# Threshold attention in one kernel: the last group's queries picked out of resident tiles by one-hot products, one index instruction per group, and a new order of steps

## The chip, the cores and the metric

The kernel runs on one core of a Trainium2 chip. The metric is the device time of one execution in microseconds (us). Five engines matter: TensorE (PE) multiplies matrices, VectorE (DVE) and ScalarE (ACT) work on tiles, GpSimd (POOL) does small vector work and issues indirect DMAs (row gathers and scatters by a list of indices), and SyncE (SP) issues plain DMAs. PEld is TensorE's loading of weights.

## The reference

```python
def reference(Q, K, V, threshold):            # 8 x 12 x 512 x 64, threshold 0.1
    scale = 1.0 / np.sqrt(Q.shape[-1])
    scores = np.einsum('bhqd,bhkd->bhqk', Q, K) * scale
    weights = np.exp(scores - np.max(scores, axis=-1, keepdims=True))
    weights = weights / (np.sum(weights, axis=-1, keepdims=True) + 1e-10)
    weights = np.where(weights > threshold, weights, 0)
    weights = weights / (np.sum(weights, axis=-1, keepdims=True) + 1e-10)
    return np.einsum('bhqk,bhkd->bhqd', weights, V)
```

With random inputs few of the 512 weights of a query exceed 0.1. Most output rows are zero.

## The kernel before

The kernel uses that sparsity. The 96 heads are 48 pairs (`hp`, two heads); two pairs share one load (`q`, 24 of them), and four pairs form a group (`x`, 12 groups, 0 to 11). The work has three layers.

**For each load**: `k` and `q` bring K and Q in (SP's queue, L324 and L328); `qcast` (L314 on POOL, L312 on DVE) makes Q 16-bit; `ktr` and `qtr` (PE, L344 and L353) transpose; `kev` and `qev` (ACT L310 or DVE L312) copy the transposes out of PSUM, `kh` makes a 16-bit K; `bits` (DVE, L383) and `norms` (PE, L435) bound the vectors' norms; `z` (SP, L546) writes zeros over the output. K stays in float32, transposed, in the tiles `kt`.

**For each pair**: for each of four key tiles `t`, `sc` (PE, L393) makes scores in one of three double PSUM banks (`two`) and `ex` takes their exponential into a 16-bit tile `e`, on ACT (L402) or as an integer trick on DVE (L404). `g` (PE, L413: 32 products) sums the pair's four `e` tiles against a small weight matrix in one of two single PSUM banks (`one`), so that the sign of a maximum (`mx`, DVE, L419) says which queries may have a weight over the threshold.

**For each group**, the candidates, up to 32 for each pair, are treated exactly: `flags` (L425), `rank` (PE, L441 and L443) and `key` (L447) number them, `oh` (L452) makes one-hot columns, `idx` (PE, L463) multiplies these by row numbers. `idxev` (L467) and `base` (L472) write the indices. Then POOL's `gather` (L475) fetches the 128 query rows from memory, `split` (L481) puts each in its head's half, `xtr` (PE, L486) transposes, `xev` copies the result to `xq`, `xqk` (PE, L496, float32, four products side by side) scores them against `kt`, `xexp` (ACT, L501), `xcut` (L506) and `xkeep` (L510) find the kept key, `xvi` (L516) and `xoi` (L521) make the index of the V row and of the output row, and POOL's `gv` (L525) and `scatter` (L534) move that row of V to the output.

Group 11 comes last, and its steps stand one after the other at the kernel's end; only its `flags`, `rank`, `key` and `oh` are in two parts (pairs 0 to 2, pair 3).

At the end four `check` steps on DVE (L652, L653, L657, L658, L661) test that no pair had more than 32 candidates and no query more than one kept key; L669 (PE), L671 and L673 reduce the answer to one number, which every engine loads (L674) to branch to a slow loop or past it. The last barriers follow (L746).

Every step's place and, where it has a choice, its engine come from `ORDER`, a coded list of 1,080 entries that is read from first to last:

```python
        for i, choice in table:
            name, engs, deps, fn, takes, gives, mode = self.ops[i]
            for pool, key in takes:
                if (pool, key) not in self.held:
                    self.held[pool, key] = idle[pool].pop(0)
            pin(lambda: fn(engs[choice]))
```

`pin` fixes the order on each engine, so that an instruction that waits holds back all behind it on its engine. `fill` steps (PE, L550, two products of 512 columns on a tile of zeros) are also placed by the list. Decoded, the end of the old list is, engine by engine (`ex.47.2` is key tile 2 of pair 47):

```
PE   ... idx.9 g.42 sc.41.3 sc.43.1 sc.41.2 qtr.23 sc.45.2 sc.45.1 g.43 g.41 sc.45.3 sc.46.3 sc.45.0
     norms.10 xtr.9 rank.10 sc.47.3 sc.44.1 sc.46.1 g.45 sc.44.3 xqk.9 sc.47.0 sc.46.0 sc.46.2 idx.10
     g.44 sc.47.2 sc.47.1 g.46 g.47 rank.11.0 norms.11 rank.11.1 fill idx.11 fill xtr.10 fill xqk.10
     fill xtr.11 fill xqk.11 and 7 fill steps
ACT  ... ex.43.3 ex.43.2 ex.43.1 qev.23 ex.45.1 ex.45.3 ex.46.3 xev.9 ex.47.3 ex.44.1 ex.44.3 xexp.9
     ex.46.0 ex.46.2 ex.47.1 xev.10 xexp.10 xev.11 xexp.11
DVE  ... idxev.9 base.9 mx.42 ex.41.3 ex.41.2 ex.45.2 mx.43 mx.41 flags.10 ex.45.0 xkeep.8 key.10
     ex.46.1 xvi.8 mx.45 oh.10 xoi.8 ex.47.0 idxev.10 base.10 mx.44 ex.47.2 mx.46 flags.11.0 bits.23
     mx.47 key.11.0 flags.11.1 oh.11.0 key.11.1 oh.11.1 split.10 idxev.11 xcut.9 base.11 xkeep.9 xvi.9
     split.11 xcut.10 xkeep.10 xvi.10 xoi.10 xoi.9 check.1 xcut.11 xkeep.11 xvi.11 check.2 xoi.11
     check.0 check.3
POOL ... gather.9 scatter.6 kh.47 split.9 gv.8 gather.10 scatter.8 gather.11 gv.9 gv.10 scatter.9
     gv.11 scatter.10 scatter.11
```

## Time and profile before

| what | us |
|---|---|
| three runs | 198.43, 194.99, 198.74 |
| their median | 198.43 |
| the profiled execution's own time | 197.65 |
| its span, first to last instruction | 195.9 |

Of the span PE is busy 91%, DVE 84%, ACT 81% and POOL 53%. A busy PE is not PE at its peak, since the ends of its pipelined matmuls are modelled. A row of the timeline gives start, duration, engine, line, operation, tiles written and read, and a count where several were merged; in brackets stand the idle time before it and what ended that. Such a releaser is inferred, and of several the last by time is named.

### The profile page before, as it was taken

To read this page: it belongs to the slowest core of one execution; us is meant where nothing else is said; L and a number is where in the kernel's file an instruction comes from. 1 tells how busy PE (TensorE), PEld (TensorE's weight loads), DVE (VectorE), ACT (ScalarE), POOL (GpSimd) and SP (SyncE) were. 2 spreads that over 40 slices of the span, in tenths; PEclk is the share of its full clock that TensorE was granted. 3 is DMA by queue.
4 is the path that set the end of the run, shared out by engine and by line. 5 is a ranking of instruction groups with operands and counts; after the bars stand their busy time and mean duration, and the time that the engine had idled before them with its cause. 6 is when DMAs were issued, how large, how long until landed. Compare 5 with 4: busy or idle time off the path is not lost.

```text
span 195.9 us, 7813 instructions
## 1 busy us (share of the span) xinstructions
PE 177.8 (91%) x3256; PEld 112.0 (57%) x3270; DVE 165.1 (84%) x322; ACT 158.7 (81%) x191; POOL 103.4 (53%) x172
## 2 busy tenths in 40 slices
PE   7999989899989989999899999999899999999730
PEld 2447557656665646666566664766377656574200
DVE  5388999789887978998899999999899999985550
ACT  2799989689989888899799989999899998961200
POOL 5386566451284740475694645759662566243560
PEclk9999999999999999999999999999999999999995
DMA  5999999998959999979879999910690000000000
GB/s 169 274 311 250 278 264 275 309 273 198 272 194 319 360 291 358 301 210 296 240 225 310 375 295 322 282 48 5 177 359 16 12 1 10 3 11 0 9 6 9
DMA packets 68023, 38.77 MB, mean 198 GB/s; under 512 B 52356, under 2 KB 64720, under 8 KB 67984
## 3 DMA queue, kind: packets, MB, share of 16 engines
q1 hardware_dynamic: 66288, 37.23, 65.3%
q0 software_dynamic: 1152, 0.47, 1.0%
q8 instruction: 27, 0.44, 1.0%
q10 hardware_dynamic: 544, 0.52, 0.8%
q14 instruction: 12, 0.10, 0.1%
HBM read 25.95 MB, written 12.98 MB: 199 GB/s over the span
## 4 chain that ended last, share of the span: by engine, by line
PE 41%; DMA 21%; DVE 14%; POOL 7%; issue 6%; ACT 6%; SPq 1%; POOLq 0%; DVEq 0%; ACTq 0%
PE two L393 13%; PE one L413 11%; DMA q<-in_Q_dram 8%; DMA k<-in_K_dram 7%; DVE e L404 5%; DMA qs<-in_Q_dram,idx 5%; ACT e L402 4%; PE one L435 4%; POOL qh L314 3%; PE two L344 3%; PE one L496 3%; PE one L353 2%; PE one L463 2%; POOL qk L314 2%; PE one L550 2%
## 5 line engine op out<-in xcount | busy, mean ns | idle before, releaser
L402 ACT ACTIVATE e<-two 128x1024 bf16<-128x1024 f32 x131 | 126.7, 1032 | 10.0 <-PE two L393 7.9
L404 DVE TENSOR_SCALAR e<-two 128x1024 int16<-128x1024 f32 x61 | 74.2, 1218 | 10.0 <-PE two L393 7.6
L393 PE MATMUL two<-qk 64*128 64x512 f16 x384 | 61.4, 381 | 1.8 <-DVE e L404 0.2
L413 PEld LDWEIGHTS <-e 128*128 128x128 bf16 x1536 | 42.2, 96 | 10.6 <-issue 10.1
L413 PE MATMUL one<-gw,e 128*128 128x48 bf16 x1536 | 46.4, 183 | 0.5 <-DVE qk L312 0.3
L314 POOL CAST qh<-q 128x512 f16<-128x512 f32 x43 | 28.1, 670 | 15.0 <-DMA q<-in_Q_dram 9.4
L314 POOL CAST qk<-kt 128x512 f16<-128x512 f32 x42 | 27.1, 657 | 9.1 <-ACT kt L310 5.3
L393 PEld LDWEIGHTS <-qk 64*128 64x128 f16 x384 | 17.2, 94 | 23.5 <-issue 14.9
L475 POOL DMA_INDIRECT qs<-in_Q_dram,idx x12 | 14.2, 1186 | 27.2 <-DVE idx L467 10.4
L419 DVE TENSOR_REDUCE st<-one 128x8 f32<-128x320 f32 x48 | 22.9, 481 | 1.4 <-PE one L413 1.3
L550 PE MATMUL one<-spare 128*128 128x512 bf16 x66 | 20.2, 406 | 1.9 <-DVE spare L187 1.3
L310 ACT COPY kt<-two 128x1024 f32<-128x1024 f32 (+1 forms) x22 | 21.4, 979 | 0.6 <-PE two L344 0.5
L525 POOL DMA_INDIRECT vr<-in_V_dram,idx x12 | 12.6, 1049 | 12.8 <-DVE idx L516 8.4
L344 PEld LDWEIGHTS two<-identity_f,k 64*128 64x128 f32 x384 | 14.7, 138 | 7.6 <-ACT e L402 3.8
L344 PE MATMUL two<-identity_f,k 64*128 64x64 f32 x384 | 17.3, 227 | 1.7 <-DMA k<-in_K_dram 1.1
L383 DVE TENSOR_SCALAR v<-qk 128x1024 int32<-128x1024 int32 x24 | 17.5, 729 | 0.0
L312 DVE COPY qk<-one 128x1024 f16<-128x1024 f16 (+1 forms) x21 | 14.1, 670 | 3.5 <-PE one L353 3.3
L534 POOL DMA_INDIRECT out_dram<-vr,idx x12 | 12.9, 1075 | 7.6 <-DVE idx L521 4.5
L353 PE MATMUL one<-identity_h,qh 128*128 128x128 f16 x192 | 14.9, 220 | 0.4 <-POOL qh L314 0.3
L353 PEld LDWEIGHTS <-qh 128*128 128x128 f16 x192 | 11.2, 97 | 5.3 <-issue 3.3
L550 PEld LDWEIGHTS <-spare 128*128 128x128 bf16 x80 | 6.4, 102 | 11.7 <-issue 7.9
L435 PEld LDWEIGHTS <-v 128*128 128x128 bf16 x384 | 10.9, 96 | 3.7 <-issue 3.4
(79 smaller groups left out, 142.7 us busy)
## 6 DMA issues: line engine op xcount, KB each, us to landing
k<-in_K_dram SPq DMA_DIRECT2D x96, 128.0 KB, 4.5
out_dram<-zero SPq DMA_DIRECT2D x24, 512.0 KB, 5.8
q<-in_Q_dram SPq DMA_DIRECT2D x23, 512.0 KB, 5.6
q<-in_Q_dram ACTq DMA_DIRECT2D x2, 256.0 KB
qs<-in_Q_dram,idx POOLq DMA_INDIRECT x12, 4.7
vr<-in_V_dram,idx POOLq DMA_INDIRECT x12, 3.2
out_dram<-vr,idx POOLq DMA_INDIRECT x12, 2.8
```

The costliest lines, as they stand in the source:

```text
L310: nc.scalar.copy(dst, src)
L314: nc.gpsimd.tensor_copy(dst, src)
L344: nc.tensor.matmul(dst[:, i, c:c + D], lhsT=src[ps, n0 + n, r, :], rhs=identity_f32[ps, ps], is_transpose=True, start=True, stop=True)
L353: nc.tensor.matmul(dst[:, c:c + P], lhsT=src[:, n0 + n, r, :], rhs=identity_h[:], is_transpose=True, start=True, stop=True)
L383: nc.vector.tensor_scalar(v_b[at("v", q)][:].rearrange("p a n c -> p (a n c)").bitcast(i32), qk_b[at("qk", q)][:].rearrange("p a n c -> p ...
L393: nc.tensor.matmul(dst[:, h, :], lhsT=qk[ps, 1, n, t * P:(t + 1) * P], rhs=qk[ps, 0, n, :], start=True, stop=True)
L402: nc.scalar.activation(dst, src, ACTF.Exp, scale=scale)
L404: nc.vector.tensor_scalar(dst.bitcast(i16), src, scale * LOG2E * 128.0, 127.0 * 128.0, op0=ALU.mult, op1=ALU.add)
L413: nc.tensor.matmul(dst[:, c * GW:(c + 1) * GW], lhsT=e_b[at("e", (hp, t))][:, h, qt * P:(qt + 1) * P], rhs=gw[:, kind[hp, t], t, :], start ...
L419: nc.vector.tensor_reduce(st_b[at("st", x)][:, n, :], one[at("one", ("g", hp))][:, 0:C2 * GW].rearrange("p (c g) -> p c g", g=GW)[:, :, 0: ...
L435: nc.tensor.matmul(dst[:, c:c + 2], lhsT=v[:, w, n, r * P:(r + 1) * P], rhs=heads[:], start=True, stop=True)
L550: nc.tensor.matmul(one[at("one", ("fill", i))][:], lhsT=spare[:, 0:P], rhs=spare[:], start=True, stop=True)
```

## The change

**The last group's queries come from tiles that are in SBUF already.** For group 11 `idxev`, `gather`, `split` and `xtr` are gone. `oh` becomes four steps, one for each pair, into a float32 tile; `pick` (PE) multiplies the loaded Q tile by these columns, which gives the transposed query rows at once, 8 float32 products for each pair; `xev` and `xqk` are in two parts (pairs 0 to 2, pair 3). `idx` for the group is 32 float32 products of 6 columns instead of 8 16-bit ones of 4, and stands behind `xqk`, since only `gv` and `scatter` need its result. `flags`, `rank` and `key` are in four parts, and the norms' part of `key` is a step of its own, `size`. The Q tiles of loads 22 and 23 are held until their `pick`.

**`g` by key tile.** For pairs 44 to 47 `g` is four steps of 8 products, one for each `e` tile as it comes.

**One index instruction.** `xvi` and `xoi` become `xo`, which writes both columns; `base` has 6 columns.

**More buffers**: indices 3 to 8, V rows 3 to 6. A few constants are laid out anew (on POOL, at the start).

**A new `ORDER`** of 1,091 entries. Of the steps with a choice of engine these change: `kev` ACT/DVE 22/3 to 23/2, `qev` 4/21 to 2/23, `kh` POOL/DVE 42/4 to 44/2, `split` POOL/DVE 9/3 to 10/1, `xev` ACT/DVE 7/5 to 7/6. The exponentials stay at 131 on ACT and 61 on DVE. Both lists have 40 `fill` steps, 27 of them ahead of the last scores.

The end of the new list, decoded:

```
PE   ... idx.9 g.42 sc.43.1 sc.41.2 sc.41.3 qtr.23 sc.45.2 g.43 sc.45.1 sc.46.3 g.41 sc.45.3 sc.45.0
     norms.10 g.45.1 rank.10 sc.44.1 sc.46.1 g.45.0 xtr.9 g.45.2 g.45.3 sc.44.3 xqk.9 sc.46.2 sc.46.0
     sc.47.3 idx.10 g.44.3 g.44.1 g.44.2 g.44.0 g.46.3 g.46.2 sc.47.2 sc.47.1 sc.47.0 g.46.0 rank.11.0
     g.46.1 norms.11.0 rank.11.1 norms.11.1 g.47.3 g.47.2 g.47.1 rank.11.2 g.47.0 pick.11.0 pick.11.1
     rank.11.3 xtr.10 pick.11.2 xqk.10 pick.11.3 xqk.11.0 xqk.11.1 idx.11 and 13 fill steps
ACT  ... ex.43.2 ex.43.3 ex.43.1 qev.23 ex.45.2 ex.45.1 ex.46.3 ex.45.0 ex.45.3 ex.44.1 ex.44.3 xexp.9
     ex.47.3 ex.46.0 ex.47.2 ex.47.1 ex.47.0 xev.10 xexp.10 xev.11.1 xexp.11
DVE  ... idxev.9 xkeep.6 mx.42 base.9 ex.41.2 ex.41.3 mx.43 bits.21 mx.41 flags.10 split.9 key.10 xcut.8
     oh.10 xo.6 xev.9 ex.46.1 mx.45 ex.46.2 idxev.10 xcut.9 base.10 flags.11.1 bits.23 mx.44 flags.11.0
     bits.22 key.11.0 mx.46 oh.11.0 flags.11.2 xkeep.8 size.11 xo.8 key.11.2 key.11.1 oh.11.1 xkeep.9
     mx.47 flags.11.3 xo.9 oh.11.2 key.11.3 oh.11.3 xev.11.0 xcut.10 xkeep.10 xo.10 xcut.11 xkeep.11
     base.11 xo.11 check.2 check.0 check.1 check.3
POOL ... gather.9 scatter.3 scatter.5 kh.47 gv.6 gather.10 gv.8 split.10 gv.9 scatter.6 scatter.7
     scatter.8 gv.10 scatter.9 gv.11 scatter.10 scatter.11
```

The loads' distance from their use, in entries of the list, also changes: `k` of load 2 stands 2 entries ahead of its `ktr` before and 28 after, `q` of loads 2, 5 and 8 stand 5, 6 and 21 ahead of their first `qcast` before and 42, 20 and 65 after, `q` of loads 6 and 16 21 and 63 before and 10 and 6 after.

The core of the diff:

```diff
+    def do_g_tile(eng, hp, t):
+        dst = one[at("one", ("g", hp))]
+        k = summed[hp] = summed.get(hp, 0) + 1
+        for c in range(C2):
+            h, qt = divmod(c, SO)
+            nc.tensor.matmul(dst[:, c * GW:(c + 1) * GW],
+                                  lhsT=e_b[at("e", (hp, t))][:, h, qt * P:(qt + 1) * P],
+                                  rhs=gw[:, kind[hp, t], t, :], start=(k == 1 and c == 0), stop=(k == SO and c == C2 - 1))
...
+    def do_oh_last(eng, n):
+        nc.vector.tensor_tensor(
+            out=oh_last[:, n], in0=slot_no[:].rearrange("p s c -> p c s"),
+            in1=keys[:, NX - 1, n * C2:(n + 1) * C2].unsqueeze(2).to_broadcast([P, C2, SLOTS]), op=ALU.is_equal)
+
+    def do_pick(eng, n):
+        src, dst = q_b[at("q", NQ - 2 + n // 2)], two[at("two", ("xt", NX - 1))]
+        for r in range(SO):
+            for h in range(2):
+                nc.tensor.matmul(dst[h * D:(h + 1) * D, 0, n * SLOTS:(n + 1) * SLOTS], lhsT=src[:, 2 * (n % 2) + h, r, :],
+                                 rhs=oh_last[:, n, h * SO + r, :], start=(r == 0), stop=(r == SO - 1))
+
+    def do_xev_last(eng, n0, n1):
+        sl = slice(n0 * SLOTS, n1 * SLOTS)
+        copy(eng, xq_b[at("xq", NX - 1)][:, sl], two[at("two", ("xt", NX - 1))][:, 0, sl])
+
+    def do_idx_last(eng):
+        dst = one[at("one", ("ix", NX - 1))]
+        for n in range(4):
+            for c in range(C2):
+                nc.tensor.matmul(dst[n * SLOTS:(n + 1) * SLOTS, 0:6], lhsT=oh_last[:, n, c, :], rhs=row_nf[:, c, :],
+                                 start=(c == 0), stop=(c == C2 - 1))
...
-    def do_xvi(eng, x):
-        b = at("ix", x)
-        nc.vector.tensor_scalar(idx_b[b][:, 1:2], accs[:, x:x + 1], ix_b[b][:, 4:5], 0.0,
-                                     op0=ALU.add, op1=ALU.max)
-
-    def do_xoi(eng, x):
+    def do_xo(eng, x):
         b = at("ix", x)
-        nc.vector.tensor_scalar(idx_b[b][:, 2:3], accs[:, x:x + 1], -(FAR - S), ix_b[b][:, 1:2],
-                                     op0=ALU.max, op1=ALU.add)
+        nc.vector.scalar_tensor_tensor(out=idx_b[b][:, 1:3], in0=ix_b[b][:, 0:2], scalar=accs[:, x:x + 1],
+                                       in1=ix_b[b][:, 2:4], op0=ALU.add, op1=ALU.max)
...
+        else:
+            add(("idx", x), ("PE",), [("oh", x, j) for j in range(4)], do_idx_last, takes=[("one", ("ix", x))], mode="c")
+            stage("base", ("DVE",), s("idx") + [("const", 4)], do_base, takes=[("ix", x)], gives=[("one", ("ix", x))])
+            for j, (n0, n1) in enumerate(((0, 3), (3, 4))):
+                add(("xev", x, j), ("ACT", "DVE"), [("pick", x, n) for n in range(n0, n1)],
+                    lambda e, n0=n0, n1=n1: do_xev_last(e, n0, n1), takes=[("xq", x)], gives=[("two", ("xt", x))])
+                add(("xqk", x, j), ("PE",), [("xev", x, j)], lambda e, x=x, n0=n0, n1=n1: do_xqk(e, x, n0, n1),
+                    takes=[("one", ("xs", x))], gives=[("xq", x), ("kt", 2 * x + n0 // 2), ("kt", 2 * x + 1)], mode="c")
+            scores = [("xqk", x, 0), ("xqk", x, 1)]
```

154 lines of the change are left out of this document (89 added, 65 removed).

## The prediction

> **What bounds the kernel now.** I read first the stretches of the span, for where each engine is full.
>
> ```profile
> 17.00:90.00 73.00, 69.13 (x1359) 45.67 (x1364) 64.78 (x114) 65.66 (x77) 37.04 (x62) 1.00 0.99 279
> 140.00:160.00 20.00, 19.91 (x409) 12.76 (x406) 18.83 (x42) 19.46 (x23) 10.49 (x13) 1.00 0.39 127
> 160.00:175.00 15.00, 14.57 (x312) 9.89 (x310) 14.46 (x27) 13.75 (x19) 7.04 (x9) 1.00 0.04 8
> 175.00:190.80 15.80, 11.18 (x130) 5.21 (x128) 9.71 (x37) 1.91 (x6) 7.70 (x8) 1.00 0.02 4
> 190.80:195.90 5.10, 0.00 (x0) 0.00 (x0) 0.00 (x0) 0.00 (x0) 0.00 (x0) 0.61 0.05 12
> ```
>
> After the length come PE, PEld, DVE, ACT and POOL busy, granted clock, DMA share and GB/s. Until 90 us the DMA engines are full (0.99). Then PE, DVE and ACT are all over 90% busy until 175, and from there on stands a tail in which ACT works 1.91 of 15.80 us: one dependent chain. Who waits for whom in the full part:
>
> ```profile
> ACT e L402 <- PE two L393: 7.9, 16, 1.8
> DVE e L404 <- PE two L393: 7.6, 11, 1.3
> POOL qh L314 <- DMA q<-in_Q_dram: 9.4, 6, 2.6
> SPq L746 <- DMA out_dram<-vr,idx: 2.7, 1, 2.7
> ```
>
> ACT and DVE wait for scores rather than the other way round. Then the tail, from the last exponentials:
>
> ```profile
> 173.56 1.21 DVE L404 TENSOR_SCALAR e<-two 128x1024 int16<-128x1024 f32 x1
> 173.69 1.02 ACT L402 ACTIVATE e<-two 128x1024 bf16<-128x1024 f32 x1 [0.17 <-PE two L393]
> ...
> 178.74 0.22 DVE L467 TENSOR_SCALAR idx<-one,slot_add 128x1 int32<-128x1 f32 x1 [0.59 <-PE one L463]
> ...
> 179.23 1.48 POOL L475 DMA_INDIRECT qs<-in_Q_dram,idx  x1 [4.05 <-DVE ix L472]
> ...
> 182.23 0.29 DVE L481 TENSOR_TENSOR qb<-qs,ix 128x128 f32<-128x128 f32 x1 [2.16 <-DMA qs<-in_Q_dram,idx]
> ...
> 182.99 0.27 ACT L310 COPY xq<-one 128x128 f32<-128x128 f32 x1 [1.51 <-PE one L486]
> ...
> 183.31 1.06 PE L496 MATMUL one<-kt,xq 128*32 128x512 f32 x8
> ...
> 183.90 0.99 POOL L525 DMA_INDIRECT vr<-in_V_dram,idx  x1 [1.89 <-DVE idx L521]
> ...
> 185.19 1.01 POOL L534 DMA_INDIRECT out_dram<-vr,idx  x1 [0.30 <-issue]
> ...
> 185.40 0.75 DVE L510 SCALAR_TENSOR_TENSOR junk<-xe,sums,key_no 128x512 bf16<-128x512 f32 x1
> ...
> 186.68 1.02 POOL L525 DMA_INDIRECT vr<-in_V_dram,idx  x1 [0.48 <-DVE oks L658]
> ...
> 189.42 0.14 DVE L673 TENSOR_SCALAR over_i<-ok 1x1 int32<-1x1 f32 x1
> 189.80 0.99 POOL L534 DMA_INDIRECT out_dram<-vr,idx  x1 [0.76 <-DVE over_i L673]
> ```
>
> and three pieces of the chain of waits:
>
> ```profile
> 184.49 0.70 ACT xe L501 x2
> ...
> 186.20 0.21 DVE idx L516
> ...
> 188.69 0.39 PE one L669 x2
> ```
>
> The last exponential ends at 174.77, the last `scatter` starts at 189.80, 15.0 us later, and the span ends 6.1 us after that (195.90 - 189.80). `scatter` follows its `gv` by 3.12 us, the row's flight; the row names L673, but by the plan `scatter` waits for `gv`. The chain from `idxev` to `xqk` by way of the gathered rows takes 183.31 - 178.74 = 4.6 us; that is what the change cuts out. SP waits 2.7 us for the last scatter, so the answer of the `check` steps (189.56) may come 2.7 us later before it matters.
>
> **The main part.** Costs of what the change touches:
>
> ```profile
> L402 ACT ACTIVATE e<-two 128x1024 bf16<-128x1024 f32 x131 | 126.7, 1032 | 10.0 <-PE two L393 7.9 <-DVE st L419 0.7 <-DVE flags L425 0.3
> L312 DVE COPY kt<-two 128x1024 f32<-128x1024 f32 x3 | 3.7, 1225 | 0.5 <-PE two L344 0.5
> L312 DVE CAST qk<-kt 128x512 f16<-128x512 f32 x4 | 2.4, 611 | 0.0
> L312 DVE COPY qk<-one 128x1024 f16<-128x1024 f16 x20 | 13.6, 682 | 0.9 <-PE one L353 0.7
> L310 ACT COPY qk<-one 128x1024 f16<-128x1024 f16 x3 | 3.1, 1026 | 0.1
> L521 DVE TENSOR_SCALAR idx<-accs,ix 128x1 int32<-128x1 f32 x12 | 2.4, 204 | 0.0
> L452 DVE TENSOR_TENSOR oh<-slot_no,keys 128x256 f16<-128x256 bf16 x1 | 0.3, 291 | 0.0
> L383 DVE TENSOR_SCALAR v<-qk 128x1024 int32<-128x1024 int32 x24 | 17.5, 729 | 0.0
> L419 DVE TENSOR_REDUCE st<-one 128x8 f32<-128x320 f32 x48 | 22.9, 481 | 1.4 <-PE one L413 1.3
> ```
>
> DVE loses 12 x 0.20 (`xoi`), one `kev` (1.2) and two `kh` (1.2), gains two `qev` (1.4); two `split` go and one `xev` comes, each near 0.29. For group 11 it gains some 1.2 in split `oh`, `flags` and `key` (0.29 for one `oh` of 256, about `xoi`'s 0.20 for a small one) and loses an `idxev` (0.2): about 2.7 us less in all. ACT loses two `qev` for one `kev`, 1.0 us less. PE's work is the same but for the tail. POOL's first constants grow by a few small ones beside a wait for the first loads; nothing.
>
> More is moved than removed. A common mark is group 9's `idxev`:
>
> ```profile
> 160.62 2.91 ACT L402 ACTIVATE e<-two 128x1024 bf16<-128x1024 f32 x3
> ...
> 161.79 0.20 DVE L467 TENSOR_SCALAR idx<-one,slot_add 128x1 int32<-128x1 f32 x1
> ```
>
> From there both lists have 17 score steps and 19 exponentials left. Of these the old one gives ACT 12, the new one 15. Exponentials back to back take 0.97 (2.91 / 3). So ACT's rest is 15 x 0.97 + 1.0 (`qev`) + 0.7 (`xexp`) = 16.3 against 13.6 (12 of them, the same two and an `xev` of 0.27), 2.6 more to a tenth. The old one took 12.9 (161.79 to 174.71), with its first exponential begun; the new one then takes 15.5. Ahead of the mark ACT has 1.0 + 2.6 = 3.6 us less work, DVE its 2.7 less (three exponentials fewer behind the mark, 3.6, are made up there by one `xkeep`, two `bits` and the parts of group 11), PE none less. So the mark comes 0 to 3.6 us earlier: nothing if PE or the loads set the pace (PE 19.91 of 20), all of it if ACT and DVE do. I take two thirds, 2.4, since ACT and DVE are at 94 to 97% there and PE's busy time covers its gaps. The last exponential then ends at 161.8 - 2.4 + 15.5 = 174.9. Call that E.
>
> **The tail.** DVE's last exponential, `ex.46.2`, is ahead of `g.46.2`, which PE must do before the scores of `ex.47.2`, `ex.47.1` and `ex.47.0`, all on ACT: 2.9 us of exponentials, scores and `g` 1.4. So DVE is free at E - 4.3. From there to `xo.9` stand 22 instructions: two `bits` 1.5, three `mx` 1.4, two `xkeep` 1.6 (185.40 to 186.20 for one), and fifteen small ones near 0.20, 3.0; 7.5 in sum: E + 3.2. POOL has `gv.9` at E + 3.5, and behind it in its queue `scatter.6`, `.7`, `.8`, `gv.10`, `scatter.9`, then `gv.11`. One indirect DMA follows another by 1.29 (183.90 to 185.19), so `gv.11` starts no earlier than 3.5 + 6 x 1.3 = E + 11.3.
>
> Along the data: `oh.11.3` is ready at E + 4.0, but PE first does `pick.11.2` and `xqk.10`. A `pick` is 8 float32 products; L496 shows two records for each, so 16, and the nearest rows give bounds:
>
> ```profile
> 18.14 0.71 PE L344 MATMUL two<-identity_f,k 64*128 64x64 f32 x16
> 168.58 0.86 PEld L413 LDWEIGHTS <-e 128*128 128x128 bf16 x32 [0.24 <-issue]
> 184.31 3.19 PE L550 MATMUL one<-spare 128*128 128x512 bf16 x13
> ```
>
> 27 (0.86 / 32) to 44 ns (0.71 / 16) a record, so 0.43 to 0.71 us. I take 0.6: `pick.11.3` ends near E + 5.9, `xev.11.1` behind `xexp.10` on ACT near 6.5, `xqk.11.1` near 7.5, `xexp.11` 8.3, `xkeep.11` 9.4. Meanwhile `idx.11`, 64 records, takes 1.7 to 2.8 on PE: 9.2 to 10.3. `base` and `xo` then end at E + 9.7 to 10.8, and with 0.27 for POOL's start (178.96 to 179.23) `gv.11` could start at 10.0 to 11.1. The queue's 11.3 is later: **POOL takes the place of the gather.** `scatter.11` is at 11.3 + 3.12 = E + 14.4 and the span's end at E + 20.5.
>
> There is a rule against this step. The Trainium skill's page "FP8 and Floating Point Precision", TensorE Precision Notes, says that true float32 takes four passes through the array. If each pass of `idx.11` were a record, 128 at 27 ns, it would end at E + 11.0, `gv.11` start at 11.8 and the end come 0.5 us later. The trace's two records for each product of L496 speak for the smaller number.
>
> Behind `idx.11` PE has all 13 fill steps, 26 products of 0.245 (3.19 / 13), 6.4 us, before L669 can test the answer: E + 15.6 to 16.7, and 0.9 on to `over_i` (188.69 to 189.56). The scatter allows it until 14.4 - 0.2 + 2.7 = 16.9. So 0 to 0.7 is added; I take 0.2, and an end at E + 20.7 = 195.6. The span of 195.9 belongs to 197.65, so 1.75 lies around it: **197.4 us**, against 197.65 now and a median of 198.43 (runs 194.99 to 198.74).
>
> **The rivals.** *Faster, 25%:* ACT and DVE set the pace, the mark comes 3.6 us early (E 173.7), and `gv.11` waits for its data alone (10.1): end 173.7 + 10.1 + 3.12 + 6.1 = 193.0, time 194.8. Loads 2, 5 and 8, which now stand further ahead of their use, may take up to 2 of the 9.4 us in which POOL's casts wait for Q. For it: the DMA share of 0.99 early on; against: loads 6 and 16 stand nearer. 192.8 to 194.8, 194.0 in the middle.
>
> *Slower, PE or loads set the pace, 15%:* the mark stays, E = 161.8 + 15.5 = 177.3, and ACT's three added exponentials are simply serial. End 198.0, time 199.8. The 7.9 and 7.6 us of waits for scores speak for it. A load that comes late at its new place costs up to one flight more:
>
> ```profile
> q<-in_Q_dram SPq DMA_DIRECT2D x23, 512.0 KB, 5.6
> ```
>
> Then 197.4 + 5.6 = 203. Holding the Q tiles of loads 22 and 23 for `pick` leaves loads 21 and 23 less room among three buffers; I put that at nothing, since DMA is idle there (0.39 and 0.04), and at this flight if it is not.
>
> *Slower, the clock falls in the tail, 10%:* the old tail has fills between its steps and the clock stays at 1.00; where PE has nothing (last stretch) it is 0.61. The new list puts all fills behind `idx.11`. At half the clock `xqk.10`, two `pick`, `xqk.11` and `idx.11` take some 1.1 + 1.2 + 1.0 + 1.7 more, 4 to 5 us on the data's path, of which the queue's lead hides one: 201 to 202. It decides from a granted clock of about 0.7 between E and E + 10. The Trainium skill, "TensorE: Matmul & The Clock Gate", Part 1, lets the clock fall after an idle window of some 3.4 us; PE's gaps above are about 1 us, and by that rule it would stay up and the time remain 197.4. No run yet shows which.
>
> *It does not do as it says, 1%:* a count over 32 sends the kernel into its slow loop, and the time is many times as long.
>
> **The numbers.** My case, no change within measurement, has 49%, its own range 195 to 200. About 2% is what runs of this kernel can tell from no change (its three spread by 1.9%): below 194.5 is faster, above 202.4 slower. Faster: most of the first rival, 0.19, and 0.02 of my case. Slower: half of the clock, a third of the second rival, 0.05 of mine and the slow loop: 0.16. The range 193.5 to 201.5 leaves out about a tenth at each end.
>
> **What would show it.** Right: no L475 in the last 20 us; L525's last start set by POOL's own chain of indirect DMAs 1.3 us apart, with `xo.11` done before; ACT's last three exponentials serial with DVE on small steps; the last exponential near 175. Wrong: an early end of the exponentials (under 173.5) or a late one (over 177); L525's last start straight behind the index instruction; a granted clock under 1.00 in the tail; SP no longer waiting for the scatter but for L673.

## The result and the profile after

| kernel | us, median (lowest to highest) | profiled execution: own time, span |
|---|---|---|
| before, same chip | 198.32 (194.99 to 201.75, 8 runs) | 197.65, 195.9 |
| changed | 207.31 (204.35 to 210.38, 8 runs) | 208.4, 206.7 |

The ratio is 1.046, with a 95% interval of 1.039 to 1.053: slower. Ratios and intervals in this document compare only the faster executions of each kernel (of the changed one the four from 204.35 to 206.21), medians are over all, and the profiled execution of 208.4 is one of the four slower ones. The forecast was 197.4 with a range up to 201.5, so it was wrong.

Three points split the profiled execution as the prediction did: the mark (group 9's `idxev`), E (the end of the last exponential) and the end.

| us | forecast | measured | off by |
|---|---|---|---|
| mark | 159.4 | 167.63 | +8.2 |
| E less mark | 15.5 | 15.36 | -0.1 |
| end less E | 20.7 | 23.7 | +3.0 |

So the working from the mark to E held; the part ahead of the mark and the last steps did not. First the part ahead of the mark. Two rows of the waits of the whole span of the changed kernel, by engine (what waited, for whom, us in all, times, longest):

```profile
PE two L350 <- DMA k<-in_K_dram: 7.7, 5, 4.8
...
SPq L812 <- PEq L744: 2.1, 1, 2.1
```

and the first of them in the kernel before:

```profile
PE two L344 <- DMA k<-in_K_dram: 1.1, 3, 0.4
```

TensorE waits 7.7 us for K; before it was 1.1, the longest 0.4. (The second row belongs to the end, below.) The timeline says where (start, duration, engine, line, operation; in brackets the idle time before and its releaser):

```profile
67.60 7.59 SPq L330 DMA_DIRECT2D k<-in_K_dram  x8
...
71.40 1.07 PE L539 MATMUL one<-kt,xq 128*32 128x512 f32 x8
77.27 0.69 PE L350 MATMUL two<-identity_f,k 64*128 64x64 f32 x8 [4.81 <-DMA k<-in_K_dram]
```

The eight DMAs of SP's row are the K loads 15 and 12, in this order; the transpose that waits is load 12's. Then the same stretches of both kernels, of the changed one first (from:to, length, PE, PEld, DVE, ACT, POOL busy, granted clock, DMA share, GB/s):

```profile
60.00:72.50 12.50, 12.46 (x225) 7.60 (x223) 11.70 (x20) 12.27 (x15) 5.12 (x8) 1.00 0.98 287
72.50:77.30 4.80, 0.03 (x2) 0.06 (x3) 0.98 (x3) 1.00 (x3) 2.72 (x3) 1.00 1.02 233
77.30:82.00 4.70, 4.43 (x86) 3.37 (x86) 1.28 (x2) 1.94 (x2) 1.17 (x2) 0.50 0.98 332
82.00:90.00 8.00, 8.00 (x143) 5.16 (x143) 6.64 (x12) 6.84 (x7) 4.01 (x5) 0.87 0.97 309
```

and of the kernel before:

```profile
72.50:77.30 4.80, 4.51 (x109) 3.28 (x106) 4.32 (x10) 4.24 (x7) 0.00 (x0) 1.00 1.11 323
77.30:82.00 4.70, 4.51 (x88) 2.88 (x87) 4.24 (x12) 4.62 (x6) 2.08 (x2) 1.00 1.06 327
```

TensorE does nothing for 4.8 us, and its clock is at half for the 4.7 us after that: PE looks busy there (4.43), but VectorE and ScalarE get 1.28 and 1.94 us of work, where they had 4.24 and 4.62. The DMA engines are full in both kernels. From group 2's `idxev` to group 3's it takes 20.6 us (64.87 to 85.50), before 14.0 (64.21 to 78.22): 6.6 us are lost here. Against the kernel before, the mark is 5.84 us late (161.79 to 167.63), as the other stretches together win 0.8; the rest of the 8.2 is the gain of 2.4 that was forecast.

The end of the changed kernel:

```profile
180.14 2.85 ACT L408 ACTIVATE e<-two 128x1024 bf16<-128x1024 f32 x3 [0.20 <-PE two L399]
...
187.91 1.94 PE L539 MATMUL one<-kt,xq 128*32 128x512 f32 x8
...
190.77 2.27 PE L539 MATMUL one<-kt,xq 128*32 128x512 f32 x8
192.48 2.22 PE L499 MATMUL one<-row_nf,oh_last 128*32 128x6 f32 x64
194.64 5.79 PE L589 MATMUL one<-spare 128*128 128x512 bf16 x26
...
194.94 0.22 DVE L560 SCALAR_TENSOR_TENSOR idx<-ix,accs 128x2 int32<-128x2 f32 x1
195.44 1.26 POOL L564 DMA_INDIRECT vr<-in_V_dram,idx  x1 [0.97 <-DVE ok_acc L722]
198.32 0.99 POOL L573 DMA_INDIRECT out_dram<-vr,idx  x1 [0.31 <-DMA vr<-in_V_dram,idx]
200.35 0.38 PE L735 MATMUL one<-identity_f,oks 128*1 128x128 f32 x2
201.08 0.14 DVE L739 TENSOR_SCALAR over_i<-ok 1x1 int32<-1x1 f32 x1
```

and stretches of it:

```profile
183.00:185.00 2.00, 1.42 (x43) 1.21 (x39) 1.67 (x8) 0.00 (x0) 1.39 (x2) 1.00 0.00 0
185.00:188.00 3.00, 2.13 (x45) 1.77 (x45) 2.51 (x8) 0.27 (x1) 1.14 (x2) 0.76 0.03 6
188.00:191.00 3.00, 3.00 (x27) 1.24 (x30) 0.59 (x3) 0.80 (x3) 2.37 (x3) 0.50 0.03 3
191.00:194.60 3.60, 3.60 (x72) 2.47 (x66) 1.56 (x5) 0.77 (x3) 2.68 (x3) 0.67 0.02 3
```

The clock is down from 185 to 194.6, and the eight records of an `xqk` (two for each product) take 1.94 and 2.27 us instead of 1.06. Yet the last `scatter` starts at E + 15.3, as before (189.80 - 174.71 = E + 15.1). What is late is the answer: 26 fill products stand ahead of L735, `over_i` comes 2.8 us behind the last `scatter`'s start, and SP now waits for PE's sequencer (2.1 us, L812), not for the scatter. The span ends 8.4 us after the scatter's start, before 6.1.

### The profile page after: what moved, and what is told of

The parts are those of the page before. It is cut to its first block, busy times and chain, and to the rows that moved or that the text cites. A ratio compares the mean times of both kernels' runs of the same rounds, so it can differ in the third digit from the quotient of the medians.

```text
span 206.7 us, 8077 instructions
## 1 busy us (share of the span) xinstructions
PE 188.2 (91%) x3405; PEld 119.8 (58%) x3405; DVE 165.5 (80%) x317; ACT 159.1 (77%) x190; POOL 103.7 (50%) x176
## 4 chain that ended last, share of the span: by engine, by line
PE 62%; DVE 13%; DMA 8%; issue 6%; POOL 3%; ACT 3%; SPq 1%; POOLq 0%; DVEq 0%; ACTq 0%
PE two L399 18%; PE one L419 13%; PE one L589 6%; DMA k<-in_K_dram 6%; DVE e L410 5%; PE two L350 5%; PE one L539 5%; PE one L359 4%; PE one L453 3%; DMA qs<-in_Q_dram,idx 2%; PE one L506 2%; ACT e L408 2%; DVE qk L318 1%; POOL qk L320 1%; PE one L431 1%
## 5 line engine op out<-in xcount | busy, mean ns | idle before, releaser
L419 PEld LDWEIGHTS <-e 128*128 128x128 bf16 x1408 | 39.3, 96 | 8.4 <-issue 7.8
L419 PE MATMUL one<-gw,e 128*128 128x48 bf16 x1408 | 43.1, 184 | 0.0
L320 POOL CAST qk<-kt 128x512 f16<-128x512 f32 x44 | 27.9, 652 | 22.2 <-ACT kt L316 20.0
L320 POOL CAST qh<-q 128x512 f16<-128x512 f32 x43 | 27.2, 654 | 15.0 <-DMA q<-in_Q_dram 7.2
L399 PEld LDWEIGHTS <-qk 64*128 64x128 f16 x384 | 18.0, 94 | 23.7 <-issue 15.5
L518 POOL DMA_INDIRECT qs<-in_Q_dram,idx x11 | 13.9, 1261 | 33.4 <-DVE idx L510 19.4
L316 ACT COPY kt<-two 128x1024 f32<-128x1024 f32 (+1 forms) x23 | 22.4, 978 | 10.1 <-PE two L350 8.9
L589 PE MATMUL one<-spare 128*128 128x512 bf16 x80 | 22.9, 412 | 1.4 <-DVE spare L188 1.3
L389 DVE TENSOR_SCALAR v<-qk 128x1024 int32<-128x1024 int32 x24 | 18.6, 781 | 0.1
L318 DVE COPY qk<-one 128x1024 f16<-128x1024 f16 (+1 forms) x23 | 15.2, 659 | 1.9 <-PE one L359 1.8
L359 PE MATMUL one<-identity_h,qh 128*128 128x128 f16 x192 | 15.3, 223 | 0.1
L539 PE MATMUL one<-kt,xq 128*32 128x512 f32 x96 | 14.9, 681 | 0.0
L359 PEld LDWEIGHTS <-qh 128*128 128x128 f16 x192 | 11.3, 99 | 5.3 <-issue 4.8
```

What stands on the lines that cost most here:

```text
L316: nc.scalar.copy(dst, src)
L320: nc.gpsimd.tensor_copy(dst, src)
L359: nc.tensor.matmul(dst[:, c:c + P], lhsT=src[:, n0 + n, r, :], rhs=identity_h[:], is_transpose=True, start=True, stop=True)
L389: nc.vector.tensor_scalar(v_b[at("v", q)][:].rearrange("p a n c -> p (a n c)").bitcast(i32), qk_b[at("qk", q)][:].rearrange("p a n c -> p ...
L399: nc.tensor.matmul(dst[:, h, :], lhsT=qk[ps, 1, n, t * P:(t + 1) * P], rhs=qk[ps, 0, n, :], start=True, stop=True)
L419: nc.tensor.matmul(dst[:, c * GW:(c + 1) * GW], lhsT=e_b[at("e", (hp, t))][:, h, qt * P:(qt + 1) * P], rhs=gw[:, kind[hp, t], t, :], start ...
```

## The experiments

In the tables "end - sc" is the time from the last `scatter`'s start to the span's end. Times are in us, ratios are against the kernel before on the same chip. Its median there was 202.2 in the first group of runs and 197.5 to 197.7 in the others, so times of different groups aren't compared. Marks, E and the ends come from one profiled execution of each kernel, the median from all.

**First group: one load, and the end.** Load 12's K ahead of load 15's, by a swap of two places in the list:

```diff
 entry 376:  k 15  ->  k 12
 entry 382:  k 12  ->  k 15
```

> The changed kernel with two loads of K exchanged in the order: load 12's ahead of load 15's, nothing else. Theory 1 (one late load makes PE stand still from 72.5 to 77.3 us, after which the clock is granted at half; the 6.6 us by which group 3's index step is late are this): the wait of L350 for k shrinks from 4.8 to about 1 us, the granted clock between 77 and 82 stays near 1.00, and the time falls by 4 to 6.5 us, to 199 to 201 where the changed kernel stands at 205. Rival (the DMA engines are full there, so whatever is exchanged the same bytes have to come): the stall moves to another load and the time falls by less than 1.5 us.

Seven of the thirteen end fills (6, 5, 9, 10, 25, 34, 37) spread over the tail, into double banks, so that they don't take the two single ones; they stand behind `norms.11.1`, `g.47.1`, `pick.11.0`, `pick.11.1` (two), `xtr.10` and `xqk.11.0`:

```diff
+    TAIL_FILLS = (6, 5, 9, 10, 25, 34, 37)
...
+        pool = "two" if i in TAIL_FILLS else "one"
```

> The changed kernel with 7 of the 13 fill steps behind idx.11 moved between the steps of the tail (into banks of the double pool), 6 left at the end. Theory 1 (the tail's few narrow products let the clock fall, and the fills behind idx.11 hold up the test of the answer): granted clock 1.00 from 180 us to the end of idx.11, L539's eight records in 1.06 us where they took 1.94 and 2.27, and the answer ready well before the last scatter lands; 3.1 us less, of which 2.3 are the answer and only 0.8 the clock, since POOL's queue of indirect DMAs then holds the last gv. Rival A (the clock is what costs, POOL's queue does not bind): 5 us less. Rival B (the clock falls in spite of the fills): 2.3 us less, L539 still at 1.9 us and more.

All thirteen left out:

```diff
-        for _ in range(2):
+        for _ in range(0 if i in END_FILLS else 2):
```

> The changed kernel without the 13 fill steps behind idx.11 (they write nothing that is used). Theory 1: the clock in the tail is as low as in the changed kernel, L735 runs as soon as the check steps are done, SP waits for the last scatter again, and the span ends 6.1 us behind the last scatter's start instead of 8.4: 2.3 us less. Rival (the answer's way through PE does not set the end): 0 us.

The spread fills, and on POOL `scatter.6` and `.7` behind `gather.10`, `scatter.8` and `.9` between `gv.9` and `gv.10`:

```diff
-gather.10 gv.8 split.10 gv.9 scatter.6 scatter.7 scatter.8 gv.10 scatter.9 gv.11
+gather.10 scatter.6 scatter.7 gv.8 split.10 gv.9 scatter.8 scatter.9 gv.10 gv.11
```

> The second kernel, and on POOL scatter.6 and scatter.7 moved up behind gather.10, scatter.8 and scatter.9 between gv.9 and gv.10, so that only gv.11 stands behind gv.10. Theory 1 (POOL's queue takes over as soon as the clock holds): 1.5 to 2.5 us less than the second kernel, the last gv straight behind xo.11. Rival A (the data sets the last gv anyway): the same as the second kernel within 0.5.

| run | median | ratio (interval) | mark | last scatter | end - sc |
|---|---|---|---|---|---|
| load 12 first | 212.35 | 1.053 (1.044 to 1.062) | 168.07 | E + 17.3 | 8.4 |
| fills spread | 208.87 | 1.038 (1.027 to 1.049) | 169.19 | E + 16.8 | 4.9 |
| no end fills | 208.92 | 1.032 (1.021 to 1.044) | 169.58 | E + 17.5 | 5.0 |
| spread, POOL reordered | 210.81 | 1.042 (1.030 to 1.054) | 169.28 | E + 18.7 | 4.8 |

The first is a miss for the theory and a hit for its rival: group 2 to 3 fell from 20.6 to 16.2 us, but group 4 to 5 rose from 21.7 to 24.8, so the stall moved. In the second and third the end is 4.9 and 5.0 us behind the last scatter, where the first, with its fills ahead of the answer, has 8.4; what that is worth in time can't be told, since the four intervals overlap. Without any wide products the clock stayed down to the end; in the second run, with some spread, it stayed at 1.00. The fourth failed: POOL's queue, freed, gave nothing, since the data of `gv.11` were ready only at E + 15.5 there. Its clock had fallen, in spite of the spread fills: to 0.58 and 0.56 from 186 to 190 us, behind a wait of TensorE's of 1.25 us.

**Second group: the order of K's loads, and the old order.** All loads of K in the order in which they are transposed, in the places that they had:

```diff
-k  ... 6 9 7 14 8 10 11 13 15 12 18 19 16 22 17 20 21 23
+k  ... 6 7 9 8 11 10 12 14 13 15 16 18 17 19 20 21 22 23
```

> The changed kernel, with the sixteen-plus loads of K issued in the order in which they are transposed; the places of the loads in the order, and everything else, stay. Theory (loads 14, 13 and 15, issued far ahead of their use, hold three of the four buffers of K, so that load 12 is issued too late and TensorE stands still for it, then runs at half its clock): TensorE's longest wait for K falls from 4.81 us to under 1.5 us, the mark of group 3 comes 5 to 7 us earlier (85.5 to about 79), and the time falls to a ratio of 1.00 to 1.025 against the kernel before. Rival (the bytes of the DMA engines set the pace, or the products of this stage in the new order do): the wait moves to another load, the mark of group 6 moves by less than 2 us, and the ratio stays at 1.035 to 1.055.

The same with the fills spread:

> The changed kernel with both edits: loads of K in the order of their use, and seven of the thirteen idle products of the end spread over the tail. If the two losses are separate, this is g1's time less 1 to 3 us, a ratio of 0.99 to 1.015; if the loss of the main part only moves (the rival of the run with K in the order of use alone), 1.025 to 1.045.

The new code under the old list: each new step takes the place of the one that it replaces, and the end is put in order by hand (`pick.11.0` to `.2`, a fill, `pick.11.3`, a fill, `xtr.10`, `xqk.11`, two fills, `xqk.10`, `idx.11`):

```diff
-xvi.9 ... xoi.9
+xo.9
-idx.11 fill xtr.10 fill xqk.10 fill xtr.11 fill xqk.11
+pick.11.0 pick.11.1 pick.11.2 fill pick.11.3 fill xtr.10 xqk.11.0 xqk.11.1 fill fill xqk.10 idx.11
```

> The code of the change (group 9's queries by one-hot products, pair by pair, one index instruction per group, last sums by key tile) under the order of the kernel before: loads, transposes, products and groups stand where they stood, only what the change puts in place of old steps is put in their place. Theory (the code is sound and the new order costs the time): a ratio of 0.985 to 1.00, mark of group 9 at 160 to 163 us, scatter of group 11 at 187 to 190 us. Rival (the one-hot products and the pair-by-pair tail cost the time themselves): a ratio of 1.02 or more, with the end 23 us or more behind the last exponential's end.

The kernel before with K in the order of use:

```diff
-k  ... 5 7 6 9 8 11 10 16 14 12 17 13 15 18 20 19 21 22 23
+k  ... 5 6 7 9 8 11 10 12 14 13 15 16 18 17 19 20 21 22 23
```

> The kernel before with nothing changed but the order of its loads of K, put into the order of their use. Theory (far-ahead loads that hold K's buffers cost time where TensorE waits for K, 4.02 us at 69 us here too): 0 to 3 us less, a ratio of 0.985 to 1.00, with the wait at 69 us below 3 us. Rival (the order of K's loads doesn't matter as long as the same bytes come): a ratio of 0.995 to 1.005 and the wait at 69 us within 0.5 us of 4.02.

(The 4.02 us in the last of these expectations is no wait of TensorE's: before, its longest for K is 0.4. Only the time of that run speaks.)

| run | median | ratio (interval) | group 3 | group 5 | mark | end - E |
|---|---|---|---|---|---|---|
| K in order | 206.65 | 1.043 (1.030 to 1.055) | 76.16 | 116.44 | 165.49 | 23.3 |
| K in order, fills spread | 202.65 | 1.029 (1.020 to 1.039) | 76.28 | 114.24 | 163.47 | 19.8 |
| new code, old order | 206.29 | 1.046 (1.038 to 1.054) | 81.15 | 112.57 | 165.33 | 22.6 |
| before, K in order | 195.76 | 0.989 (0.980 to 0.998) | 75.15 | 106.71 | 159.48 | 21.8 |
| (before) | 197.69 | | 78.22 | 109.14 | 161.79 | 21.2 |
| (changed) | 207.31 | 1.046 | 85.50 | 118.60 | 167.63 | 23.7 |

With K in order the stall for load 12 is gone, group 3 comes 9.3 us sooner than in the changed kernel, and the ratio hardly changes (1.046 to 1.043). The next stall, in the run with K in order alone (GpSimd's queue and SP's in the timeline):

```profile
77.05 1.13 SPq L334 DMA_DIRECT2D q<-in_Q_dram  x1
78.22 2.34 SPq L585 DMA_DIRECT2D out_dram<-zero  x3
80.66 5.92 SPq L330 DMA_DIRECT2D k<-in_K_dram  x4
86.68 1.47 SPq L334 DMA_DIRECT2D q<-in_Q_dram  x1
...
92.33 0.84 POOL L320 CAST qh<-q 128x512 f16<-128x512 f32 x1 [8.23 <-DMA q<-in_Q_dram]
```

The first `q` is load 15, the second load 13, which is used first. It stands behind load 15, three zero stores and a K load, and POOL waits 8.2 us for it. This goes back to the changed list of Q loads (`... 12 11 14 15 13 20 16 ...`). The two runs with K in order, without and with the fills spread, show the end once more: the last `scatter` starts at E + 15.1 and E + 15.0, the ends lie 8.2 and 4.8 us behind it.

The new code under the old order missed its expectation by far. Its mark is 3.5 us later than before, 1.5 of them there already at group 0, and its hand-made end takes 22.6 us from E where the expectation had 23 or more as the rival's sign. So the rival's ratio held. This order was not made for these steps, so it doesn't show what the code alone costs under an order of its own.

**Third group: the zero stores and Q.** Twelve zero stores (groups 6 to 11, 6.3 MB) behind the last load, with K in order and the fills spread (the other twelve keep to places among the loads, but in the order of their groups); then Q in the order of use too; then the kernel before and the new code under the old order with K in order and late zero stores:

```diff
 h1:  z.12 ... z.23, until now among the loads, behind k 23, seven entries apart
 h2:  h1, and
-q  ... 10 12 11 14 15 13 20 16 17 18 19 22 21 23
+q  ... 10 11 14 12 13 15 16 17 18 19 20 22 21 23
```

> The changed kernel with K in the order of use and the fills spread, as in the run before it, and besides the twelve zero stores of groups 6 to 11 (6.3 MB) moved behind the last load of K. Theory (a load of Q that TensorE's next products need stands on SP's queue behind zero stores, and GpSimd waits 8.2 us for it): the stretch from group 3's mark to group 6's, 49.2 us in that run, falls by 2 to 5 us, and the ratio from 1.029 to 1.005 to 1.02. Rival (the zero stores fill idle DMA time only): the stretch stays within 1.5 us and the ratio within 0.6% of 1.029.

> As h1, with the loads of Q in the order of their use too (load 13 in the place of load 15, ahead of three zero stores). Theory (the second stall is load 13 of Q, issued behind load 15, as the first was load 12 of K behind 15): no wait of GpSimd for Q over 4 us between 76 and 117 us, group 5's mark at 106 to 110 us, and a ratio of 0.985 to 1.01. Rival (the new order of products is slow by itself): group 5's mark at 113 us or later and a ratio of 1.02 or more.

> The kernel before with its loads of K in the order of use and the twelve zero stores of groups 6 to 11 behind the last load. If DMA requests set the pace of the kernel before too, 1 to 4 us less than with K in order alone, a ratio of 0.965 to 0.985; if that kernel is paced by its engines, within 1 us of it, 0.983 to 0.995.

> The new code under the old order, with the same two edits to its loads. If the loss of 4.6% of the new code under the old order came from late loads, it falls to within 1% of b2. If the code costs it (six instructions more at the start, narrower products, the pair-by-pair end), it stays 3% or more above b2.

**Fourth group: which of them.** On the changed kernel K and Q in order alone; late zero stores alone; all load edits with the fills at the end; and h2 with `xkeep.9` and `xo.9` behind `xev.11.0` and with `scatter.6`, `.7` and `.8` ahead of the later `gv`:

> The changed kernel with nothing moved but the loads of K and of Q, each put into the order of use in the places they had; the zero stores and the fills stay. If the order of the loads alone makes the main part late, the mark of group 9 comes at 157 to 161 us as in h2 and the ratio is 1.01 to 1.025 (what is left is the slow clock of the end). If a load still stands too long behind zero stores, the mark of group 9 stays at 163 us or later and the ratio at 1.03 or more.

> The changed kernel with nothing moved but the twelve zero stores of groups 6 to 11, behind the last load; K and Q stay in the changed order. If the zero stores ahead of the loads make them late, TensorE's wait for K at 72 us falls below 2 us, the mark of group 3 comes at 77 to 80 us and the ratio is 1.00 to 1.02. If it is three of K's four buffers held ahead of use (load 12 can only be issued when one is free), the stall between groups 2 and 3 stays, that mark comes at 82 us or later, and the ratio is 1.025 or more.

> As h2 (K, Q in the order of use, late zero stores) with the thirteen fills back at the end, as the change has them. If the fills' place costs what the end showed before, the end comes 22.5 to 24 us behind the last exponential, with a clock of 0.5 to 0.8 there, and the ratio is 1.010 to 1.02; if the slow clock of the end came with the stalls of the main part, the end is within 1 us of h2's 19.7 us and the ratio within 0.5% of 0.999.

> h2 with its tail in another order: the count of group 9 (two instructions of 0.92 us together that stand ahead of the last group's maximum on VectorE) behind the last group's queries, and three scatters (1.3 us each) ahead of the gathers of values on GpSimd's queue. Expected: the last maximum ends 0.9 us earlier and the whole 0.5 to 1.5 us, a ratio of 0.990 to 0.996. Rival (GpSimd's queue is not late and VectorE only shifts its work): within 0.3% of h2's 0.999.

| edits on the changed kernel | median | ratio (interval) | group 3 | group 5 | mark | end - E |
|---|---|---|---|---|---|---|
| late zeros | 204.09 | 1.039 (1.031 to 1.048) | 79.47 | 112.39 | 163.75 | 22.4 |
| K, Q | 203.39 | 1.029 (1.019 to 1.039) | 75.19 | 109.17 | 162.20 | 23.6 |
| K, Q, late zeros (i3) | 202.27 | no interval | 75.96 | 108.02 | 161.02 | 26.0 |
| K, late zeros, fills (h1) | 198.45 | 1.005 (1.001 to 1.009) | 76.20 | 109.44 | 162.61 | 21.1 |
| K, Q, late zeros, fills (h2) | 197.76 | 0.999 (0.994 to 1.004) | 75.09 | 107.26 | 158.39 | 19.7 |
| h2 with its tail reordered (j1) | 197.02 | 0.997 (0.992 to 1.002) | 76.97 | 109.34 | 160.98 | 19.5 |
| before, K and late zeros (b2) | 197.28 | no interval | 75.97 | 107.03 | 160.52 | 20.9 |
| new code, old order, K and late zeros (c2) | 202.82 | 1.029 (1.021 to 1.037) | 78.37 | 109.04 | 161.99 | 25.5 |

What follows. (1) The loss comes with the list, not with the new steps alone: with four edits, to the places of K's and Q's loads, of the zero stores and of the fills, the same code takes the time of the kernel before (0.999, 0.994 to 1.004). Whether it would lose a little against a kernel before whose loads are mended as well was not measured side by side; that kernel's ratio with K in order is 0.989 in one run and 0.996 in the other. (2) No edit alone does it. Late zero stores and K's order each take the first stall away (group 3 at 79.5 and 76.2 instead of 85.5); the stalls behind it then decide. Late zeros added to K's order and spread fills are worth 2.4% (1.029 to 1.005). Q's order on top, 1.005 to 0.999, can't be told from nothing, since the intervals overlap. (3) What the fills' place costs in time is less clear. With K in order, spreading them took the ratio from 1.043 to 1.029, and these intervals overlap too; with all loads mended and the fills at the end (i3), four executions lie between 197.7 and 204.3, too far apart to be set against h2. In the traces the end takes 23.3 us with the fills at the end and 19.8 with them spread, and 26.0 (i3, the slowest of the four) against 19.7 (h2). (4) The two predictions for "which one" were both half right: K and Q in order gave a mark of 162.2 between the two announced bands, late zeros gave the early group 3 of the one theory and the ratio of the other. (5) K's order and late zeros together gave the kernel before nothing that can be seen (197.28 against 197.48, no interval). (6) Under the old order the new code still loses 2.9%, and its median is 2.8% above that of the kernel before with the same edits (202.82 against 197.28): late loads don't explain its loss. Its hand-made end takes 25.5 us where the other's takes 20.9, with the clock at 0.50 to 0.73 between 178 and 187 us.

Where h2 gets it back, in its stretches from group 3 to 5 and from 5 to 7:

```profile
76.00:107.30 31.30, 30.62 (x602) 20.21 (x600) 30.24 (x50) 28.42 (x35) 18.35 (x25) 1.00 0.82 246
107.30:131.20 23.90, 23.90 (x480) 15.75 (x479) 22.69 (x43) 22.42 (x28) 13.18 (x18) 1.00 0.63 152
```

PE is busy 98 to 100% and the clock stays up. In the run with K and Q in order but the zero stores among them, PE once waits 1.9 us for a cast of POOL's, and pays for longer:

```profile
114.56 0.60 PE L399 MATMUL two<-qk 64*128 64x512 f16 x4 [1.94 <-POOL qk L320]
```

```profile
112.00:115.00 3.00, 1.06 (x18) 0.42 (x15) 1.50 (x4) 1.40 (x2) 2.27 (x3) 1.00 1.17 311
115.00:118.00 3.00, 2.83 (x55) 1.82 (x54) 2.44 (x5) 2.35 (x3) 1.09 (x2) 0.66 0.86 161
118.00:121.00 3.00, 3.00 (x21) 0.65 (x19) 2.28 (x4) 1.64 (x2) 1.93 (x2) 0.50 0.62 130
```

The end of h2, with nothing late:

```profile
184.39 1.42 POOL L573 DMA_INDIRECT out_dram<-vr,idx  x1 [0.31 <-issue]
186.11 1.04 POOL L564 DMA_INDIRECT vr<-in_V_dram,idx  x1 [0.30 <-DVE ok L721]
...
188.71 0.14 DVE L743 TENSOR_SCALAR over_i<-ok 1x1 int32<-1x1 f32 x1
188.76 0.99 POOL L573 DMA_INDIRECT out_dram<-vr,idx  x1 [0.30 <-issue]
```

`xo.11` ends at 185.27, and `gv.11` starts only at 186.11, one indirect DMA behind `scatter.9`: here POOL's queue binds, by 0.6 us, if POOL's start of 0.27 is counted. The answer and the last scatter come together, and the span ends 4.7 us later (6.1 in h1, where SP waited 2.4 us for the scatter to land, here 0.7). j1 took `gv.11` from E + 12.35 to E + 11.8 and the time by an amount that its interval can't tell from none.

**Fifth group: a last attempt, and the best kernel.** j1 with `ex.46.0` on DVE and `xkeep.8`, `xo.8` behind `flags.11.3` (on POOL `split.10` also moves ahead of `gv.8`); and the kernel before with K in order once more, beside it:

```diff
-ACT: ex.47.3 ex.46.0 ex.47.2      DVE: base.10 flags.11.1
+ACT: ex.47.3 ex.47.2              DVE: base.10 ex.46.0 flags.11.1
```

> j1 with one of the fifteen exponentials that ScalarE runs behind the mark of group 9 (of pair 46, 1.03 us) given to VectorE, and the count of group 8 moved behind the last pair's flags to make room for it. If ScalarE's chain sets the last exponential's end (mark of group 9 plus 15.4 us), that end comes at the mark plus 14.2 to 14.6 us, and the whole is 0.4 to 1.2 us shorter than j1, a ratio of 0.990 to 0.995. If VectorE takes its place as the bound, the last exponential's end comes earlier but the end keeps its place, and the ratio stays at 0.996 to 1.00.

> The kernel before with its loads of K in the order of use, side by side with j2 on one chip. If its gain of 1.1% is the K loads' order, the ratio is 0.985 to 0.993 again; if it was the spread of that chip's runs, 0.995 to 1.005.

The first (j2) took 200.98, ratio 1.011 (1.003 to 1.020): a miss. E is still the mark + 15.37 (160.28 to 175.65), since ScalarE now waits instead. What grew is the part behind E, 24.0 us where j1 takes 19.5: TensorE's clock fell, though the fills are spread, and VectorE waits 2.65 us for its products (three views of that run, the second a stretch):

```profile
172.79 2.86 ACT L408 ACTIVATE e<-two 128x1024 bf16<-128x1024 f32 x3 [1.12 <-PE two L399]
```

```profile
176.00:178.00 2.00, 2.00 (x38) 1.45 (x35) 0.53 (x3) 0.00 (x0) 0.33 (x1) 0.50 0.01 2
```

```profile
179.19 0.24 DVE L465 TENSOR_TENSOR keys<-one,flags 128x8 bf16<-128x8 f32 x2 [2.65 <-PE one L461]
```

The second took 196.55, ratio 0.996 (0.993 to 1.000), against 0.989 (0.980 to 0.998) the first time: the intervals overlap. The second value is what the expectation named for a mere spread of the runs, and the gain, if any, is under 1%. It and j1 are the best found, 0.3 to 0.4% under the kernel before; j1's interval holds 1.

## Why the prediction was wrong

**The main part: wrong, and here the forecast fell.** The step that failed is "So the mark comes 0 to 3.6 us earlier: nothing if PE or the loads set the pace". The mark came 5.84 us later than before, for TensorE stood 4.81 us for a load, and 6.6 us were lost between groups 2 and 3. That sentence let the loads set the pace, but took for granted that the new list brings none of them later than the old one. A late load stood in the second rival at "one flight more", 5.6 us, with 15% for the whole rival, and was looked for among loads 2, 5, 8, 6, 16, 21 and 23. It was load 12 of K, and behind it, once that was mended, load 13 of Q. What was not read out of the list is the order in SP's queue: K loads 14, 13 and 15 are issued far ahead of their use, hold three of the four buffers, and load 12, needed first, can only follow when a buffer comes free, behind zero stores on a full queue. It takes both: the old list also has loads 16 and 14 ahead of 12, without a wait over 0.4 us, and with the zero stores late and K's order as changed this stall went too. The trace of before had the sign of it, a DMA share of 0.99 until 90 us. That the price of 6.6 us is near the 5.6 that were named is luck: it is no flight, but 4.8 us of standing and then half the clock. With all loads mended the mark is 158.4 in h2, 160.3 in j2 and 161.0 in i3 and j1. That is 0.8 to 3.4 us earlier than before and inside the 0 to 3.6, but h2's value is from the fastest of its ten executions, and the 2.4 that were taken are not confirmed.

**From the mark to E: right.** 15.36 us measured, 15.36 and 15.37 in j1 and h2; in the four runs of the first group, on a slower chip, it was 16.4. The reason given, ScalarE's fifteen exponentials in a row, is not all of it: with fourteen (j2) the time stayed, as TensorE's scores come next.

**POOL takes the place of the gather: not in the changed kernel, and right in h2.** No L518 stands in the last 20 us. `gv.11` starts at E + 12.45 where E + 11.3 was forecast. In the changed kernel POOL stands idle for 0.97 us ahead of it and starts it straight behind the index instruction (`xo.11` ends at 195.16, `gv.11` starts at 195.44), which the prediction named as a sign of being wrong: the data come last. With the clock up the data come 0.65 us sooner, and in h2 the queue holds `gv.11` until E + 12.35. A `pick` takes 0.66 at full clock (0.6 taken), `idx.11` 2.2 (1.7 to 2.8). `oh_last` takes 0.61 where 0.29 was measured for a 16-bit result: four times 0.3 more on VectorE. The last scatter is at E + 15.3, forecast 14.4; it gains nothing on the old E + 15.1.

The float32 rule of the page "FP8 and Floating Point Precision" (the Trainium skill, TensorE Precision Notes), four passes, would have meant 128 records if each were one. The row of `idx.11` shows 64 records for its 32 products, in 2.2 us; the smaller number held.

**The answer: the term that was mis-sized.** "0 to 0.7 is added; I take 0.2." The fills ended at E + 17.4 and `over_i` came at E + 18.1 against a limit of 16.9, and the limit itself was wrong. The prediction took SP's wait of 2.7 us for slack. But where the answer comes last, the end is 4.6 us (no end fills) to 5.6 us (changed kernel) behind `over_i`; of the 6.1 us from the scatter to the end that leaves the answer 0.5 to 1.5 us behind the scatter's start, not 2.5. So the end was 8.4 us behind the scatter: 2.3 more than before, and 3.5 to 3.6 more than in five of the runs with the fills spread. In the two others, h1 and j2, SP waited 2.4 and 2.7 us for the scatter to land, and the end was 6.1 and 6.3 us behind it, so part of the difference is the scatter's landing.

**The clock falls in the tail: the rival's mechanism came true, with another price.** It fell to 0.50 to 0.76, as its condition said. But the data's path lost little by it: `xo.11` ends at E + 12.2 in the changed kernel and E + 11.9 in the run with K in order, both with the clock down, and at E + 11.5 with it up (the run with K in order and the fills spread). The last scatter starts at E + 15.1 in the one and E + 15.0 in the other of these two runs with K in order. `idx.11`, and the fills behind it, came later: it ends at E + 11.7 where 9.2 to 10.3 was forecast. Where it lasted to the end (no end fills) the scatter was at E + 17.5, against E + 17.3 and E + 16.8 in the two runs on that chip with load 12 first and with the fills spread: 0.7 us at most, where 4 to 5 were priced.

**The forecast's own time.** 197.4 is near what h2 takes (197.76), with the loads in time and the clock up, and there its three terms are 158.4, 15.4 and 19.7 us against 159.4, 15.5 and 20.7. But the kernel before takes 197.48 on that chip, so the two agree on no change and no more, and these terms are from h2's fastest execution. The forecast took for granted what the new list does not give.

## What to carry to other kernels

Before costing a new order, list what stands on each DMA queue in the order of issue beside the order of use: a load that is issued ahead of one that is needed sooner holds a buffer and a place in the queue, and every edit that mends one stall is only worth what the next one leaves. Look at what an idle product, or any work moved to the end, puts ahead of the last answer, and measure the slack of that answer from the end of the program, not from a wait. A list that is tuned as a whole can't be judged by one of its parts: here four separate edits were needed to see that the new steps can run in the old time, and no order was found in which they gain.

## What the hardware showed that was not expected

**The clock falls without a long gap.** The Trainium skill, "TensorE: Matmul & The Clock Gate", Part 1, has the clock fall after an idle window of some 3.4 us. Here a wait of 1.94 us was followed by 0.66 and 0.50 for some 6 us (above). And in the end of the run with all loads mended and the fills at the end no wait of PE's from E (176.49) to 181 was over 0.39 us, while the clock went down:

```profile
160.00:176.00 16.00, 15.87 (x359) 11.17 (x356) 14.41 (x34) 15.26 (x18) 6.72 (x6) 1.00 0.04 8
176.00:178.00 2.00, 1.81 (x51) 1.66 (x49) 1.66 (x7) 0.49 (x1) 0.91 (x1) 0.74 0.00 0
178.00:181.00 3.00, 2.61 (x46) 2.29 (x44) 2.93 (x9) 0.27 (x1) 1.39 (x3) 0.50 0.03 6
```

In the run with the fills spread alone PE was less busy, and the clock stayed up:

```profile
191.00:194.00 3.00, 2.35 (x30) 0.77 (x30) 0.26 (x1) 0.25 (x1) 2.39 (x3) 1.00 0.03 3
194.00:197.00 3.00, 2.04 (x48) 1.43 (x47) 1.13 (x4) 0.97 (x4) 1.50 (x2) 1.00 0.01 1
```

The products differ: narrow ones (2 to 48 columns) in the first, with some of 512 columns between them in the second. But that doesn't settle it. The new code under the old order ran the same products in the same order at its end twice: with its loads as they were the clock stayed at 1.00 from E (178.61) to 195 us, and with K in order and late zero stores it fell to 0.63, 0.50 and 0.73 between 178 and 187 us. It also fell with the fills spread, in the run with POOL reordered and in j2. The four executions of the first kernel spread over 6.6 us. What decides stays open.

**The wait lay ahead of the issue.** In the run with K in order, load 13 of Q took 5.65 us from its issue to its use (86.68 to 92.33), about what any load of Q takes there (5.5 to 6.3). The 8 us were lost ahead of the issue, behind three stores that nobody waited for (2.3 us to issue them) and a K load (5.9 us), with a DMA share of 1.00 and 1.06 from 77 to 87 us. The Trainium skill ("DMA: Bandwidth & Descriptors", Queues, rings and completion order) says that each DMA engine takes up the entries of a queue's ring in order, though a later one may finish its write earlier; no run here shows the two apart.
